# A hybrid recurrence and attention layer: the stores of two stages leave SyncE for the engines that make their data, and three prompt columns of the front move from VectorE to ScalarE

## The chip, the cores and the metric

One core of one Trainium2 chip runs the whole program in a single launch. The metric is the device time of one execution in microseconds (us). Three timed executions of the kernel before took 2099.51, 2095.64 and 2098.21 us; the median is 2098.21 us. A further execution ran under the profiler and took 2093.83 us; every row of the trace is from that one.

Engine names: PE is TensorE, DVE is VectorE, ACT is ScalarE, POOL is GpSimd, SP is SyncE. A DMA is started by an engine's instruction stream: SP, ACT and POOL each have one, and each works its instructions off in order. A DMA instruction whose semaphore has not come therefore holds up what stands behind it in that stream.

## The reference, cut to what matters

The kernel computes one layer of a diffusion backbone in float32, for 1024 latent tokens and 256 prompt tokens of width 1024:

```
h = rms_norm(x) * (1 + sc1) + sh1
z = h @ w_in                      # hq, hf_fwd, hf_bwd, hi, hg, aq, ak, av, gl
q, k = rms_norm per head of aq, ak (latents: rotary positions too)
o_a = softmax(q k^T / 8) v        # latents: cached context keys and latent keys; prompt: prompt keys
f = lb + (1 - lb) * sigmoid(hf)   # gates of the recurrence, both directions
o_h = chunked gated linear recurrence(hq, f, hi), forward + backward; final state is an output
o_h = rms_norm(o_h) * silu(hg)
x = x + g1 * ((sigmoid(gl)[0] * (o_h @ w_ho) + sigmoid(gl)[1] * (o_a @ w_ao)) @ w_out)
x = x + g2 * (square(relu(norm(x) @ w_ff1)) @ w_ff2);   y = rms_norm(x)
```

The shifts, scales and gates (sh, sc, g) are products of a conditioning vector with `w_ada`, one for latents and one for the prompt. Outputs are both y, the prompt's keys and values, and the prompt's final states.

## The kernel before

Tokens are held in three tiles t: t = 0 and 1 are 512 latents each, t = 2 is the 256 prompt tokens. A float32 product is made of three matmuls on operands split in two parts (a rounded high part `hi` made by ACT, and `lo = x - hi` made by DVE): hi*hi, hi*lo, lo*hi. So each column of activations and each block of weights needs one ACT and one DVE instruction before PE can use it. `split` (L283 on ACT, L284 on DVE) does it for weights.

The stages, in order of time in the trace:

- **Front (to about 125 us).** For each tile t and each of eight columns kc (128 of the 1024 channels), PE transposes the tokens (L263), `norm1_col` makes `hs` (the hi part, ACT L272), the whole value `xnb` (ACT L276, or DVE L274 where kc % 3 == 1) and the lo part (DVE L277), and `front_z` multiplies with the weights of the second half of q, and of k and v (L561, L562, L565). Normalisation and rotary positions of q and k (`qk_norm`, L397 to L418) and the splits `qst` and `kst` run on ACT, DVE and POOL beside it. In tile 2 two sets of weights for the first half of q are split as well (`w_aq`, tile `wq`). The L565 matmul of a column needs `hs` of L277; L329 to L331 behind the last column need the `wq` splits.
- **Attention (125 to about 735 us).** First the other half of q (`z_tok`). Then units of one head and 256 queries go through scores (L697), exponentials (ACT L708), normalisation of `pexp` by POOL or DVE in turn (L716), transposes (L738), splits (`pTh`, `pTl`), and values (L754, output `oa` L763). A `Filler` puts the projections for the recurrence between these: QD, FD, VD, GD are scratch tensors in DRAM that `hq_consume`, `hf_consume`, `hi_consume` and `hg_consume` store (tile `ze`), OA takes the outputs of attention.
- **Recurrence (735 to about 1010 us).** 24 units of one head, direction and tile. `prep` loads `uf`, `uq`, `uv`, `ug` from FD, QD, VD, GD, and DVE and POOL make the decays (DVE scans L874 to L880, POOL L883 and L911, both L907). Then PE transposes the keys (`keys_t`, L936), multiplies scores (L947), states (L959; DVE L968 carries them on) and outputs. The gate projections `gl` are the filler here, stored to GT.
- **Projections and MLP (from about 1010 us).** These load OH, OA and GT, and then work through the output projection, the first and the second feed-forward product.

Every instruction's place in its engine's stream is decided before the run: a scheduler lists instructions in program order, moved ahead by `tc.high_priority(offset=...)` by so many places. The splits of `wq` stand in such a block with offset 600, as do the instructions of `norm1_col`.

A store by `dma` (L101) is an instruction of SP, by `store` (L104) one of POOL. Before the change SP issues all loads, and all stores of attention and recurrence. `with_ada` puts the products with `w_ada` (matmuls L181, ACT L183, then `late`: matmuls L188 and ACT L191) between the filler's projections; each `late` waits in the list `todo` for the next projection.

## Time and profile before

| | us |
|---|---|
| median of three timed executions | 2098.21 (2095.64 to 2099.51) |
| the profiled execution, device time | 2093.83 |
| its span in the trace | 2092.1 |
| PE busy in the span | 2035.8 |
| DVE busy | 1405.6 |
| ACT busy | 952.0 |
| POOL busy | 540.3 |

The span is the time from the first to the last instruction in the trace; 1.73 us lie around it. Issuing a DMA is not counted as busy. A row of the timeline gives the start in us, the duration in us, the engine, the line, the operation, the tile written and the tiles read, how many alike instructions follow each other, and in brackets the idle time ahead of it and what ended that. Durations of instructions that follow each other overlap a little: the step from start to start is what one costs its engine. PEclk is the share of full speed granted to PE.

### The profile page before, as it was taken

The page shows a single profiled execution, that of the slowest core. Times are in us where ns is not written, and L with a number is a line of the kernel's source. Part 1 is how long each engine was busy: PE and PEld are TensorE (multiplying, and loading weights), DVE is VectorE, ACT ScalarE, POOL GpSimd, SP SyncE. Part 2 cuts the span into 40 slices and gives each one's busy share as a digit, 9 for nine tenths or more (in the row PEclk, how much of TensorE's full clock was granted, in tenths as well). Part 3 has the DMA queues.
Part 4 walks back from the last instruction along what each step waited for, and adds up shares of the span by engine and source line. Part 5 has one row for each costly group of instructions (what it writes and reads, how often), then busy time and mean ns, then how long its engine had stood idle before and what let it go on. Part 6 is the DMA issues. An engine that isn't in the chain of part 4 may idle for free.

```text
span 2092.1 us, 33337 instructions
## 1 busy us (share of the span) xinstructions
PE 2035.8 (97%) x12244; PEld 1748.0 (84%) x12244; DVE 1405.6 (67%) x2653; ACT 952.0 (46%) x1961; POOL 540.3 (26%) x577
## 2 busy tenths in 40 slices
PE   6899999999999999999999999999999999999998
PEld 4788889988889978888888888988888888888876
DVE  4784676776776797778354735776666666577686
ACT  4754555555565522322231425654454544333442
POOL 1472232333323355455212200222211210000010
PEclk9999999999999999999999999999999999999999
DMA  9455220232221355445644523774444479545773
GB/s 295 130 165 168 74 76 31 77 116 69 78 74 37 107 164 175 139 146 158 216 145 140 206 101 99 218 215 149 157 146 156 157 254 365 166 154 177 228 252 124
DMA packets 230243, 319.19 MB, mean 153 GB/s; under 512 B 18072, under 2 KB 148720, under 8 KB 230080
## 3 DMA queue, kind: packets, MB, share of 16 engines
q1 hardware_dynamic: 217664, 277.41, 41.4%
q0 software_dynamic: 12416, 39.66, 5.3%
q8 instruction: 96, 1.57, 0.3%
q14 instruction: 67, 0.55, 0.1%
HBM read 229.43 MB, written 87.57 MB: 152 GB/s over the span
## 4 chain that ended last, share of the span: by engine, by line
PE 83%; DVE 8%; DMA 5%; ACT 2%; issue 1%; SPq 0%; POOL 0%; DVEq 0%; POOLq 0%; ACTq 0%
PE ps_g L312 7%; PE ps_g L314 7%; PE ps_g L313 7%; PE ps_s L697 4%; PE ps_t L738 4%; PE ps_g L1591 2%; PE ps_g L1589 2%; PE ps_g L1590 2%; PE ps_g L754 2%; PE ps_s L1437 2%; PE ps_s L1438 2%; PE ps_s L1439 2%; DMA wraw<-in_w_ff 2%; PE ps_g L329 2%; PE ps_g L753 2%; PE ps_g L331 2%
## 5 line engine op out<-in xcount | busy, mean ns | idle before, releaser
L312 PE MATMUL ps_g<-hs,wsp 128*128 128x512 f32 (+1 forms) x896 | 322.3, 360 | 0.1
L314 PE MATMUL ps_g<-hs,wsp 128*128 128x512 f32 (+1 forms) x896 | 309.5, 345 | 0.8 <-DVE wsp L284 0.8
L313 PE MATMUL ps_g<-hs,wsp 128*128 128x512 f32 (+1 forms) x896 | 309.0, 345 | 0.0
L716 POOL TENSOR_SCALAR pexp<-pexp,rs 128x512 f32<-128x512 f32 (+1 forms) x104 | 170.2, 1643 | 375.6 <-ACT pTh L741 190.8
L283 ACT ACTIVATE wsp<-wraw 128x1024 fp32r<-128x1024 f32 x110 | 109.6, 998 | 262.8 <-PE ps_g L313 81.0
L284 DVE TENSOR_TENSOR wsp<-wraw,wsp 128x1024 fp32r<-128x1024 f32 x110 | 134.3, 1223 | 120.8 <-ACT wsp L283 120.4
L314 PEld LDWEIGHTS ps_g<-hs,wsp 128*128 128x128 f32 x896 | 169.3, 189 | 22.7 <-DVE wsp L284 1.0
L312 PEld LDWEIGHTS ps_g<-hs,wsp 128*128 128x128 f32 x896 | 169.7, 189 | 21.2 <-issue 4.6
L313 PEld LDWEIGHTS ps_g<-hs,wsp 128*128 128x128 f32 x896 | 170.0, 190 | 15.3
L741 ACT ACTIVATE pTh<-ps_t 128x512 fp32r<-128x512 f32 x200 | 118.9, 601 | 122.3 <-PE ps_t L738 119.3
L698 DVE TENSOR_REDUCE mx<-ps_s 128x1 f32<-128x512 f32 (+1 forms) x208 | 137.0, 663 | 53.9 <-PE ps_s L697 53.4
L283 ACT ACTIVATE ah<-ar 128x640 fp32r<-128x640 f32 (+1 forms) x112 | 80.9, 723 | 187.4 <-PE ps_g L1590 102.3
L708 ACT ACTIVATE pexp<-ps_s,ngm 128x512 f32<-128x512 f32 (+1 forms) x208 | 137.4, 669 | 43.2 <-DVE ngm L702 41.7
L742 DVE TENSOR_TENSOR pTl<-ps_t,pTh 128x512 fp32r<-128x512 f32 x200 | 136.0, 681 | 15.8 <-ACT pTh L741 15.4
L284 DVE TENSOR_TENSOR ah<-ar,ah 128x640 fp32r<-128x640 f32 (+1 forms) x112 | 90.1, 805 | 77.2 <-ACT ah L283 76.0
L697 PE MATMUL ps_s<-Kl,Ql 128*128 128x512 f32 (+1 forms) x416 | 128.9, 415 | 1.6 <-ACT pexp L708 1.6
L738 PE MATMUL ps_t<-ident,pexp 128*128 128x128 f32 x800 | 120.7, 273 | 2.5 <-DVE ngm L702 1.3
L329 PE MATMUL ps_g<-wsp,hs 128*128 128x256 f32 x400 | 117.5, 294 | 0.0
L331 PE MATMUL ps_g<-wsp,hs 128*128 128x256 f32 x400 | 113.7, 284 | 0.0
L330 PE MATMUL ps_g<-wsp,hs 128*128 128x256 f32 x400 | 113.6, 284 | 0.0
L754 PE MATMUL ps_g<-pTl,Vl 128*128 128x256 f32 x400 | 106.2, 286 | 3.6 <-DVE pTl L742 3.5
L753 PE MATMUL ps_g<-pTh,Vl 128*128 128x256 f32 x400 | 106.1, 285 | 1.3 <-DVE oa L763 1.1
(417 smaller groups left out, 5443.5 us busy)
## 6 DMA issues: line engine op xcount, KB each, us to landing
ar<-AF SPq DMA_DIRECT2D x112, 320.0 KB, 3.5
wraw<-in_w_ff SPq DMA_DIRECT2D x32, 1024.0 KB, 6.4
wr<-in_w_ff SPq DMA_DIRECT2D x128, 256.0 KB, 4.5
wraw<-in_w_in SPq DMA_DIRECT2D x18, 1024.0 KB, 5.5
wraw<-in_w_ada SPq DMA_DIRECT2D x16, 1024.0 KB, 5.5
AF<-a POOLq DMA_DIRECT2D x48, 256.0 KB, 2.8
AF<-t POOLq DMA_DIRECT2D x48, 256.0 KB, 2.3
wa<-in_w_ada SPq DMA_DIRECT2D x32, 256.0 KB, 5.8
```

The lines of the kernel that those rows point to most:

```text
L283: s_.activation(hi, raw, AF.Copy)
L284: v.tensor_tensor(lo, raw, f32(hi), op=ALU.subtract)
L312: pe.matmul(out, hi[:, k, :], mh, start=(first and k == 0), stop=False)
L313: pe.matmul(out, hi[:, k, :], ml, start=False, stop=False)
L314: pe.matmul(out, lo[:, k, :], mh, start=False, stop=(last and k == kcs - 1))
L329: pe.matmul(po[:, bb, :], mh[:, off:off + P], wh[:, k % 4, :], start=(k == 0), stop=False)
L331: pe.matmul(po[:, bb, :], ml[:, off:off + P], wh[:, k % 4, :], start=False, stop=(k == KC - 1))
L697: pe.matmul(pq[:, 0:n], self.qh[:, q0:q0 + P], K[self.g][var][self.kts[i]], start=(var == 0), stop=(var == 1))
L716: NORM[(i + j) % len(NORM)].tensor_scalar(x, x, self.rs[j], None, op0=ALU.mult)
L738: pe.transpose(pt[:, a, j * P:(j + 1) * P], self.Ps[j][i][:, b * P:(b + 1) * P], ident)
L753: pe.matmul(pv[:, 0:256], V[self.g][kg][:, b, :], hi[:, a, :], start=(k == 0), stop=False)
L754: pe.matmul(pv[:, 0:256], V[self.g][kg][:, b, :], lo[:, a, :], start=False, stop=(k == last))
```

## The change

Four things are changed.

1. Stores in attention and recurrence no longer go through SP. POOL issues those of OA (12), FD (24), GD (10) and the final states (8), in all 54. ACT issues those of QD (12), VD (10), OH (12) and GT (48), in all 82, by a new helper `store_act`. SP keeps all loads, and the stores of KS, VS, QS, of the caches and of X.
2. In `norm1_col` the columns kc = 1, 4, 7 of the prompt tile (t = 2) have `xnb` made by ACT, no longer by DVE.
3. The splits of `wq` have offset 0 in place of 600.
4. `with_ada` no longer ends attention's filler with the last `late`; it is taken by the first projection of the recurrence's filler.

```diff
+    def store_act(out, in_):
+
+        s_.dma_start(out=f32(out), in_=f32(in_))
...
-            if kc % 3 == 1:
+
+            if kc % 3 == 1 and t < 2:
                 v.tensor_scalar(xn[:, 0:n], pt[:, 0:n], sc, sh, op0=ALU.mult, op1=ALU.add)
             else:
                 s_.activation(xn[:, 0:n], pt[:, 0:n], AF.Identity, scale=sc, bias=sh)
...
-            with tc.high_priority(offset=600):
+            with tc.high_priority(offset=0):
                 for j in range(2):
                     split(*[x[:, 2 * j:2 * j + 2] for x in w_aq[-1]], raw_aq[kc - 4 + j])
...
-                dma(OA[self.h // 2][self.t], o_at[self.h // 2, self.t][:, 0:n])
+                store(OA[self.h // 2][self.t], o_at[self.h // 2, self.t][:, 0:n])
...
-            dma(QD[2 * c + half][t], e[:, 0:n])
+            store_act(QD[2 * c + half][t], e[:, 0:n])
...
-            dma(FD[d][h][t], e[:, 0:n])
+            store(FD[d][h][t], e[:, 0:n])
...
-            dma(VD[c][pr // 2][:, 2 * (pr % 2):2 * (pr % 2) + 2], e)
+            store_act(VD[c][pr // 2][:, 2 * (pr % 2):2 * (pr % 2) + 2], e)
...
-            dma(GD[c][pr // 2][:, 2 * (pr % 2):2 * (pr % 2) + 2], e.rearrange("p (b h) d -> p b (h d)", b=2))
+            store(GD[c][pr // 2][:, 2 * (pr % 2):2 * (pr % 2) + 2], e.rearrange("p (b h) d -> p b (h d)", b=2))
...
-            dma(OH[self.h][self.t], e[:, 0:nb].rearrange("p b d -> p (b d)"))
+            store_act(OH[self.h][self.t], e[:, 0:nb].rearrange("p b d -> p (b d)"))
...
-                    dma(O["new_state_hgrn"][u.d, u.h], st)
+                    store(O["new_state_hgrn"][u.d, u.h], st)
...
-            dma(GT[2 * c + half][t], e[:, 0:n])
+            store_act(GT[2 * c + half][t], e[:, 0:n])
...
-        if todo:
+        if todo and b0:
             todo.pop()()
```

The added lines shift the line numbers of the changed kernel: lines 106 to 272 of before are 4 higher, those from 273 on 5 higher.

The stream of DVE in the front, before, from the last but one column's lo part (first row, L277) to the first `qst`; the last column's lo part is row 134, its `xnb` row 128, the splits of `wq` (L284) rows 129 and 131:

```order
125 L277 TENSOR_TENSOR hs<-xnb,hs 128x256
126 L411 TENSOR_TENSOR qa<-qn,cosb 128x256 x2
127 L403 TENSOR_TENSOR qn<-qn,kwb 128x256
128 L274 TENSOR_SCALAR xnb<-ps_t,s_132,modc 128x256
129 L284 TENSOR_TENSOR wsp<-wq,wsp 128x512
130 L411 TENSOR_TENSOR qa<-qn,cosb 128x128
131 L284 TENSOR_TENSOR wsp<-wq,wsp 128x512
132 L411 TENSOR_TENSOR qa<-qn,cosb 128x128
133 L402 TENSOR_TENSOR qn<-qe,qrst 128x512
134 L277 TENSOR_TENSOR hs<-xnb,hs 128x256
135 L403 TENSOR_TENSOR qn<-qn,qwb 128x512
136 L418 TENSOR_TENSOR qa<-qa,qb 128x256
```

The same place in the changed kernel (the lo parts are L282 now, the `wq` splits L289):

```order
121 L404 TENSOR_REDUCE qss<-sq 128x8
122 L416 TENSOR_TENSOR qa<-qn,cosb 128x256 x2
123 L408 TENSOR_TENSOR qn<-qn,kwb 128x256
124 L282 TENSOR_TENSOR hs<-xnb,hs 128x256 x2
125 L169 TENSOR_SCALAR ms<-qss 128x8
126 L289 TENSOR_TENSOR wsp<-wq,wsp 128x512
127 L416 TENSOR_TENSOR qa<-qn,cosb 128x128 x2
128 L289 TENSOR_TENSOR wsp<-wq,wsp 128x512
129 L485 TENSOR_TENSOR qst<-qa,qst 128x4x64
130 L423 TENSOR_TENSOR qa<-qa,qb 128x256
```

The last two lo parts follow each other directly, ahead of the last two `wq` splits; `xnb` is gone from DVE.

The stream of POOL where the recurrence begins, before (`uf`, `usf`, `uw` are tiles of a unit's `prep`, `ze` with L851 the GD data; row 80 is the L911 of the second unit):

```order
76 L911 TENSOR_TENSOR usf<-uf,usf 128x512
77 L907 TENSOR_TENSOR uw<-uq,um 128x512 x2
78 L907 TENSOR_TENSOR uf<-usf,um 128x512
79 L883 TENSOR_SCALAR uf<-uf 128x512
80 L911 TENSOR_TENSOR usf<-uf,usf 128x512
81 L891 MEMSET um 128x4x16
82 L907 TENSOR_TENSOR uf<-usf,um 128x512
83 L907 TENSOR_TENSOR uw<-uq,um 128x512 x2
84 L851 TENSOR_TENSOR ze<-ze,hnb 128x512
```

And in the changed kernel, with the stores (L104 DMA) that POOL issues between:

```order
146 L916 TENSOR_TENSOR usf<-uf,usf 128x512
147 L104 DMA GD_1_1973<-ze 128x512
148 L912 TENSOR_TENSOR uw<-uq,um 128x512 x2
149 L912 TENSOR_TENSOR uf<-usf,um 128x512
150 L104 DMA OA_2_1905<-oa 128x256
151 L888 TENSOR_SCALAR uf<-uf 128x512
152 L104 DMA OA_2_1908<-oa 128x256
153 L916 TENSOR_TENSOR usf<-uf,usf 128x512
154 L912 TENSOR_TENSOR uw<-uq,um 128x512 x2
155 L896 MEMSET um 128x4x16
156 L856 TENSOR_TENSOR ze<-ze,hnb 128x512
157 L912 TENSOR_TENSOR uf<-usf,um 128x512
```

A store of OA stands between the two instructions that make the second unit's `usf`, and its `uf` of L912 now comes behind `uw` and `ze`.

DVE's stream at the same place, before, around the `usf` (L907) of the first unit, which PE's first key transposes read:

```order
994 L284 TENSOR_TENSOR wsp<-wraw,wsp 128x1024
995 L892 COPY um<-ucp 128x4x3
996 L893 TENSOR_TENSOR um<-ucp 128x4x2
997 L763 TENSOR_TENSOR oa<-ps_g,pvt 64x256
998 L907 TENSOR_TENSOR usf<-usf,um 128x512
999 L896 COPY um<-ucp 128x4
1000 L899 RECIPROCAL um<-ucp 128x4x4
1001 L917 TENSOR_TENSOR uq<-uq,ucp 128x512
```

And in the changed kernel:

```order
990 L289 TENSOR_TENSOR wsp<-wraw,wsp 128x1024
991 L897 COPY um<-ucp 128x4x3
992 L898 TENSOR_TENSOR um<-ucp 128x4x2
993 L901 COPY um<-ucp 128x4
994 L768 TENSOR_TENSOR oa<-ps_g,pvt 64x256
995 L904 RECIPROCAL um<-ucp 128x4x4
996 L922 TENSOR_TENSOR uq<-uq,ucp 128x512
997 L912 TENSOR_TENSOR usf<-usf,um 128x512
```

Three instructions of the second unit (the copy, the reciprocal and `uq`) moved ahead of the first unit's `usf`.

## Rows read from the trace of the kernel before

**Rows 1.** The profile page, its first part: busy us of each engine, share of the span, instructions.

```profile
PE 2035.8 (97%) x12244; PEld 1748.0 (84%) x12244; DVE 1405.6 (67%) x2653; ACT 952.0 (46%) x1961; POOL 540.3 (26%) x577
```

**Rows 2.** Busy time of the engines in stretches of the program. Columns: stretch and its length, busy us and instructions of PE, PE weight load, DVE, ACT, POOL, then PEclk, DMA share, GB/s.

```profile
100.00:125.00 25.00, 20.17 (x106) 16.76 (x105) 24.21 (x56) 16.82 (x42) 18.24 (x23) 0.86 0.61 180
125.00:735.00 610.00, 603.50 (x4251) 545.24 (x4250) 417.25 (x897) 341.55 (x806) 206.30 (x139) 1.00 0.27 86
735.00:775.00 40.00, 35.22 (x267) 29.73 (x265) 39.37 (x69) 10.27 (x19) 23.96 (x24) 0.96 0.52 171
775.00:1010.00 235.00, 232.63 (x1889) 196.02 (x1887) 186.21 (x438) 64.03 (x166) 123.17 (x145) 1.00 0.51 161
...
1300.00:1420.00 120.00, 115.13 (x851) 109.43 (x849) 91.37 (x148) 74.89 (x132) 27.69 (x39) 1.00 0.70 213
```

**Rows 3.** What PE waited for over the whole span: us in total, times, longest us.

```profile
PE ps_s L565 <- DVE hs L277: 4.3, 2, 3.5
PE ps_t L263 <- ACT xnb L276: 4.0, 2, 2.9
...
PE ps_t L936 <- DVE usf L907: 3.5, 2, 1.9
```

**Rows 4.** What SP's stream waited for, in the same form (the row of the FD data).

```profile
SPq L101 <- DVE ze L833: 177.6, 21, 15.5
```

**Rows 5.** The end of the front in stretches of 3 us, columns as in rows 2.

```profile
110.00:113.00 3.00, 3.00 (x17) 2.47 (x16) 3.00 (x7) 1.75 (x3) 3.00 (x5) 1.00 0.97 293
113.00:116.00 3.00, 1.44 (x7) 0.86 (x5) 3.00 (x6) 1.22 (x2) 3.00 (x4) 1.00 0.50 159
116.00:119.00 3.00, 1.02 (x4) 0.59 (x4) 3.00 (x7) 0.62 (x3) 1.97 (x4) 0.94 0.00 0
119.00:122.00 3.00, 3.00 (x16) 3.00 (x17) 3.00 (x6) 2.35 (x9) 2.92 (x5) 0.50 0.96 309
122.00:125.00 3.00, 3.00 (x27) 3.00 (x27) 2.87 (x10) 1.50 (x5) 1.26 (x2) 0.99 0.93 220
```

**Rows 6.** PE's timeline there: the last full-speed matmul, the two that wait for the last column, and the first of the next product.

```profile
114.06 0.39 PE L562 MATMUL ps_g<-wsp,hs 128*128 128x512 f32 x1
117.98 0.50 PE L565 MATMUL ps_s<-wsp,hs 128*128 128x512 f32 x1 [3.54 <-DVE hs L277]
...
118.88 0.58 PE L329 MATMUL ps_g<-wsp,hs 128*128 128x256 f32 x1
```

**Rows 7.** DVE's timeline there; in the left-out lines DVE has no gap either.

```profile
113.28 0.53 DVE L274 TENSOR_SCALAR xnb<-ps_t,s,modc 128x256 f32<-128x256 f32 x1
113.74 0.68 DVE L284 TENSOR_TENSOR wsp<-wq,wsp 128x512 fp32r<-128x512 f32 x1
114.34 1.35 DVE L411 TENSOR_TENSOR qa<-qn,cosb 128x128 f32<-128x128 f32 x1
115.61 0.80 DVE L284 TENSOR_TENSOR wsp<-wq,wsp 128x512 fp32r<-128x512 f32 x1
...
117.39 0.54 DVE L277 TENSOR_TENSOR hs<-xnb,hs 128x256 fp32r<-128x256 f32 x1
...
118.79 0.68 DVE L480 TENSOR_TENSOR qst<-qa,qst 128x256 fp32r<-128x256 f32 x1
```

**Rows 8.** ACT's timeline in the front: a column's `xnb` of the same size on ACT, the next instruction, and ACT's wait behind it.

```profile
108.55 0.58 ACT L276 ACTIVATE xnb<-ps_t,modc,s 128x256 f32<-128x256 f32 x1
109.05 0.56 ACT L272 ACTIVATE hs<-ps_t,modc,s 128x256 fp32r<-128x256 f32 x1
110.74 0.60 ACT L488 ACTIVATE qT<-ps_t 128x512 fp32r<-128x512 f32 x1 [1.12 <-PE ps_t L485]
```

**Rows 9.** The transposes of `qst` that the product behind the front reaches (PE's timeline), the first of which reads the last row of rows 7.

```profile
126.46 0.45 PE L485 MATMUL ps_t<-ident,qst 128*128 128x128 f32 x4
```

**Rows 10.** DMA instructions by the line of the helper that issues them: count, min/median/max ns of the instruction on its stream, first and last start.

```profile
L101 SPq DMA_DIRECT2D GT<-ze x48: 319/320/601, 760.2 to 1069.2; - x48
...
L104 POOL DMA_DIRECT2D AF<-a x48: 540/540/555, 1404.4 to 1701.4; - x48
```

**Rows 11.** Timelines where the recurrence begins: DVE, then PE.

```profile
749.84 1.30 DVE L907 TENSOR_TENSOR usf<-usf,um 128x512 f32<-128x512 f32 x1
751.06 0.16 DVE L896 COPY um<-ucp 128x4 f32<-128x4 f32 x1
751.14 0.24 DVE L899 RECIPROCAL um<-ucp 128x16 f32<-128x16 f32 x1
751.30 0.62 DVE L917 TENSOR_TENSOR uq<-uq,ucp 128x512 f32<-128x512 f32 x1
...
751.20 0.66 PE L936 MATMUL ps_t<-ident,usf 128*128 128x128 f32 x4 [1.58 <-DVE usf L907]
```

**Rows 12.** Timelines in the recurrence: SP, then DVE, then PE.

```profile
893.24 0.34 SPq L101 DMA_DIRECT2D out_new_state_hgrn<-ust  x1
893.67 0.38 SPq L101 DMA_DIRECT2D uf<-FD  x1
...
896.61 1.23 DVE L878 TENSOR_TENSOR_SCAN ucp<-R,uf 128x512 f32<-128x512 f32 x1 [0.83 <-DMA uf<-FD]
...
902.11 0.63 PE L936 MATMUL ps_t<-ident,usf 128*128 128x128 f32 x4 [1.95 <-DVE usf L907]
```

**Rows 13.** POOL's timeline in attention: a `pexp` of L716 and the wait ahead of it.

```profile
506.70 1.76 POOL L716 TENSOR_SCALAR pexp<-pexp,rs 128x512 f32<-128x512 f32 x1 [3.92 <-ACT pTh L741]
```

## The prediction

> **What bounds the kernel now.** I read the page's busy times first [rows 1]: PE works 2035.8 of 2092.1 us, so all that a change can win without touching the products is 56.3 us of idle PE and what a lowered clock costs. Next I cut the span into the stages that the change touches [rows 2]. PE's idle time is length less busy: 4.83 us in the end of the front (100 to 125, at a granted clock of 0.86), 6.5 us in 610 us of attention, 4.78 us where the recurrence begins (735 to 775), 2.37 us in its rest, 4.87 us in the first feed-forward product. Attention and recurrence, where nearly all the stores are, have 13.65 us together. Third comes the list of what PE waited for [rows 3]. Three rows bear on the change: 4.3 us for the lo parts `hs` of DVE L277, of which one wait is 3.5; 4.0 us for `xnb` of ACT L276, also in the front; 3.5 us for DVE's `usf`, both in the recurrence. No wait there names a store. Fourth, SP's own waits [rows 4]: 177.6 us in 21 waits for the data of the FD stores. It is a long time, but time of a stream, not of PE; it counts only where a load behind such a store is late for PE.
>
> **The front: the last column (edits 2 and 3).** In 110 to 113 PE is full at clock 1.00; in 113 to 119 it works 1.44 and 1.02 of 3 us; then, in 119 to 122, it is full but the granted clock is 0.50, the lower of its two levels (1.2 of 2.4 GHz) [rows 5]. PE's timeline shows why: the last L562 starts at 114.06 and the next instruction, L565, at 117.98, after 3.54 us for `hs` [rows 6]. DVE's timeline shows what it did instead [rows 7]: `xnb` of that column at 113.28, a split of `wq` (0.60 us from start to start), `qa` (1.27), a second split of `wq` (0.73), two more instructions, and only at 117.39 `hs`. DVE had no gap, so this is order and load, not latency.
>
> In the changed order `xnb` is gone from DVE (0.46 us by start to start [rows 7]) and the last two `hs` stand ahead of both splits. The two `hs` stand about where `xnb` stood, and take little more (an `hs` lasts 0.54 us, `xnb` 0.53): the last is done between 113.3 and 114.2, I take 113.6, ahead of the 114.45 (114.06 + 0.39) at which PE has ended its L562 [rows 6]. So the 3.54 us go. What is late next? L329 would start about 0.9 us after L565 (118.88 less 117.98 [rows 6]), near 115.4, and needs the second set of split `wq` only for its fifth of eight blocks, 12 matmuls later; 27 of them go in 3 us at full clock [rows 5], so 1.3 us: near 116.7. Counted from 113.6, one split (0.60), two `qa` (1.27, and 0.4 at most) and the last split (0.73) [rows 7] end near 116.6. That is just in time, an estimate with nothing to spare. Without the idle time there is no reason left in these rows for the lower clock, since it was granted in full until PE had been idle: 3 us at 0.50 are worth 1.5 us. Both together are 5.0 us. Lower bound of the gain is 0 (the wait reappears elsewhere), the upper 5.0. I take 4.4, because a slack of 0.1 us is likely to leave a wait of about half a microsecond.
>
> **The front: the other two columns (edit 2).** ACT gets three `xnb` for 0.5 us each, the step from 108.55 to 109.05 [rows 8]. Behind 109.05 ACT waited 1.12 us, so the last one is hidden by that. The middle one falls where ACT is the engine PE waits for (the 4.0 us of `xnb` L276 [rows 3]), and can cost its 0.5; the first saves DVE 0.5 while PE hangs on DVE's chain, and can win as much. Sum 0, bounds -0.5 to +0.5.
>
> **Attention (edit 1).** It puts 24 FD, 12 OA and 10 GD stores on POOL, and 12 QD and 10 VD stores on ACT. SP took 0.32 us for one [rows 10]; on ACT the nearest price is that of SP, so 22 x 0.32 = 7.0 us in a stage in which ACT works 341.55 of 610 us [rows 2]. On POOL a store of this size took 0.54 us [rows 10], so 46 of them are 25 us; POOL works 206.30 of 610. Both fit in idle time. Added waits: each store on POOL waits for DVE's `ze` or `oa`, and behind it stand the `pexp` of L716, which PE's transposes read. POOL was idle 3.92 us ahead of a `pexp` [rows 13], which is the cover; ACT's stores wait for ACT's own data alone. If one in five of ACT's 22 held up a `pexp` that PE waits for, that is 4 x 0.32 = 1.3 us. On the other side, SP's freed loads could win what they cost PE now, of which rows 3 show nothing. Taken: 0; bounds -0.5 to +1.5.
>
> "Perfetto Trace Analysis" of the Trainium skill (DMA Optimizations) says that it may pay to give inputs to one issuing engine and outputs to another. Against it, the skill's "DMA: Bandwidth & Descriptors" (Issuing engines are not separate DMA queues) says that starting DMAs from several engines saves only the issuing stream's time, because all run on the same 16 DMA engines. The trace agrees with the second in attention, where SP waits 177.6 us [rows 4] and PE for no load; by the first, the third rival below would be the likeliest.
>
> **The start of the recurrence (edits 1 and 4).** DVE works 39.37 of 40 us here [rows 2], so the order on DVE decides. PE's first key transposes wait 1.58 us for `usf`, made at 749.84 [rows 11]. In the changed order a copy, a reciprocal and `uq` come first: 751.06 to 751.92, or 0.86 us by these rows. So L936 starts some 0.8 us later. POOL's OA store between L888 and L916 delays the second unit's `usf` by its wait and 0.54; PE reads it only a unit later. The two L188 that edit 4 takes from ahead of L936 give nothing, as PE waits there anyway. Taken +0.8, bounds 0 (`usf` took 1.30 us beside POOL; later it may take 0.7) and +1.5 (0.86 and a 0.6 us collision again).
>
> **The rest of the recurrence (edit 1).** The other wait for `usf`, 1.95 us at 902.11, goes back to a load [rows 12]: SP issues the store of a final state at 893.24, as soon as DVE has made it, and the load of `uf` behind it at 893.67; DVE waits 0.83 us for that load at 896.61, and is then busy until `usf`. With the store on POOL the load goes as soon as its buffer is free. At least 0.83 us of the 1.95 hang on it, at most all. Against it: POOL now waits for the state, with the L907 behind it that DVE's `usf` needs. Taken -1.0, bounds -1.95 and +1.0. ACT's 60 stores are 60 x 0.32 = 19 us beside 64.03 busy of 235 [rows 2]: nothing.
>
> **The first feed-forward product.** Its instructions stand in another order on DVE and ACT, as the scheduler's places shift. PE is idle 4.87 us there [rows 2]; 0, bounds -1.5 and +1.5.
>
> **The sum.** -4.4 + 0 + 0 + 0.8 - 1.0 + 0 = -4.6 us. The profiled execution, 2093.83 us, is 4.38 under the median of the timed ones, and the sum is made against it: 2089.2 on its scale, and 2098.2 - 4.6 = 2093.6 on the scale of the timed runs. I give the latter. Adding bounds: -5.0 -0.5 -0.5 + 0 - 1.95 - 1.5 = -9.5 and 0 + 0.5 + 1.5 + 1.5 + 1.0 + 1.5 = +6.0.
>
> **Rivals.**
> *The front's wait only moves.* DVE has no gap from 110 to 122 [rows 5], and the edits take three `xnb` of 0.46 us off it; all that was put behind `hs` must be done later. The `wq` splits were in time by 0.1 us in my count; and PE, 5 us earlier, reaches the `qst` transposes of 126.46 [rows 9] near 121.5, with `qst` done at 119.47 before [rows 7]: 2 us in place of 7. If a wait of 3.5 us appears at either, only the clock's part of the gain and the recurrence stay: -4.6 + 3.5 = -1.1, so 2097.1 us. For it: DVE's full stretches. Against it: DVE's next 25 us of the second half of q, of which PE is the bound.
>
> *POOL's head of line in attention* ends slower. Place: the FD stores, which wait for DVE behind ACT. SP stood 8.5 us for one on average (177.6 / 21 [rows 4]). If POOL stood as long, a `pexp` behind it would be late by 8.5 less the cover of 3.92, or 4.6 us, plus the store's 0.54. The point from which it decides is a wait of 3.4 us (3.92 - 0.54). Three such hits among 32 units cost 15 us: 2098.2 - 4.6 + 15 = 2108.6. For it: the streams work in order. Against it: SP came early because it had little else; POOL has 206.30 us of its own work and the stores stand behind the matmuls that make their data.
>
> *SP's freedom is worth more.* All of the 3.5 us for `usf` [rows 3] goes, and loads run ahead so far that the DVE work of the first units starts before attention ends: then -0.8 - 1.6 - 1.0 on top of the sum, -8.0, so 2090.2. Against it: DVE has 0.63 us of free time in the 40 us around the start [rows 2].
>
> *The stores leave SP and nothing follows, the front's order aside*, is the forecast itself with -4.4 + 0.8: 2094.6, inside its own range.
>
> **Chances.** Forecast 0.47, with its own range from 2091 to 2096; the wait moves 0.22; SP's freedom 0.18; POOL's head of line 0.13. About 0.2% (4.2 us) is what a measurement of this kernel tells from no change, so faster begins below 2094.0, close to the forecast. Of the forecast's 0.47 some 0.27 lie below, of SP's freedom 0.17, of the moved wait 0.03: faster 0.47. Slower than 2102.4 is POOL's rival with 0.12 and little else: 0.13; the same 0.40. The range from 2087 to 2101 leaves out most of POOL's rival and a tail of the gain.
>
> **What the profile of the changed kernel would show.** Right: in the front no PE wait above 1 us on the lo part L282, and clock 1.00 from 110 to 125; PE's first L936 wait some 0.8 us longer; the 1.95 us wait shorter. SP's list no longer names `ze` and `oa`, POOL's does. Wrong: a PE wait of over 1 us on `qst` or a `wq` split, or one on `pexp` of POOL in attention, behind a DMA of L104. The whole would be wrong if PE's idle time in attention and recurrence (13.65 us) changed by more than 3 us in either direction.

## The result and the profile after

The change made the kernel slower: 2105.2 us, the median of six executions (2103.98 to 2105.92), against 2097.02 us for the kernel before on the same chip (2094.2 to 2099.51). The ratio is 1.0038, 95% interval 1.0027 to 1.005: 8 us, between 5.7 and 10.5. Forecast were 2093.6 us, with a range from 2087 to 2101.

The profiled execution after took 2105.22 us, its span is 2103.4. Against the 2092.1 of the profile before, which lies at the low end of that kernel's times, that is 11.3 us, and these I take apart. The page's first part, to be read against [rows 1]:

```profile
PE 2036.3 (97%) x12244; PEld 1747.4 (83%) x12244; DVE 1404.2 (67%) x2650; ACT 953.1 (45%) x1964; POOL 570.1 (27%) x631
```

PE has the same 12,244 matmuls and works 0.5 us more, so the loss is time in which PE stands. POOL has 54 instructions more, its new stores: other than on SP and ACT, the issuing of a DMA does count as busy on POOL, which works 29.8 us more (0.55 us for each).

PE issues the same matmuls in both kernels in the same order (but for two of L188 that edit 4 moves), so the traces can be laid side by side: the start of the n-th matmul in one, less its start in the other. The table below cuts that difference at fixed matmuls, named by the time at which they start in the trace before. A plus is time lost against the trace before. Its kernels are those of the experiments that follow; the row "after" says where the 11.3 us are.

| us | to 96.6 | front, to 123.6 | attention, to 732.6 | start of recurrence, to 789.2 | its rest, to 1000.0 | to 1457.4 | to 2083.6 | behind the last matmul |
|---|---|---|---|---|---|---|---|---|
| after | -0.9 | -3.7 | -0.8 | +6.8 | +4.9 | +0.9 | +0.6 | +3.5 |
| e1_front_only | -1.2 | -3.7 | -1.7 | +1.6 | +1.7 | +2.6 | -0.4 | 0 |
| e2_no_pool_stores | -3.0 | -3.7 | -1.5 | +2.1 | +6.3 | +2.5 | -1.0 | 0 |
| e3_gd_on_sp | -0.8 | -3.7 | +0.6 | +2.3 | +7.4 | +1.2 | -1.2 | +2.7 |
| e4_oa_on_sp | -2.9 | -3.7 | -1.5 | +2.6 | +6.6 | +5.2 | -0.1 | +2.9 |
| e5_no_act_stores | -2.6 | -3.7 | -1.2 | +5.5 | +2.5 | +1.1 | -1.1 | +3.5 |
| e6_late_back | -0.7 | -3.7 | -1.2 | +5.6 | +6.7 | +2.3 | -1.1 | +3.5 |
| e7_front_a_on_act | -1.1 | -3.7 | -0.4 | 0 | +0.6 | +1.2 | +0.1 | +2.5 |
| e8_fd_alone_on_pool | -0.9 | -3.7 | +1.4 | +0.4 | +5.5 | +2.0 | -0.8 | +1.2 |
| e9_26_on_act | -3.4 | -3.8 | -0.8 | +1.4 | +2.1 | +2.7 | +1.8 | +4.3 |
| e10_32_on_act | +0.4 | -3.7 | -0.6 | +1.3 | +1.9 | +2.1 | +0.5 | +4.3 |
| e11_edit3_alone | -0.9 | +1.3 | -0.3 | +1.6 | +2.3 | -0.3 | -0.2 | 0 |
| e12_20_off_pool | -0.2 | -3.7 | -2.4 | +1.7 | +2.5 | +3.4 | +1.2 | -0.2 |

How fine may this be read? The first column compares mostly the same instructions and spreads by 3.8 us. e11 has the order of before in attention and recurrence, and still loses 1.6 and 2.3 there against that one profile: differences of 2 us in a stage are noise, mostly single stretches at the lower clock that one execution has and another has not. The front's column and the last one repeat to 0.1 us where the kernels agree.

**The front gained.** Stretches of the trace after, as in [rows 2, 5]:

```profile
100.00:125.00 25.00, 21.93 (x145) 18.99 (x146) 22.74 (x57) 18.29 (x45) 17.74 (x24) 1.00 0.76 235
119.00:122.00 3.00, 3.00 (x30) 3.00 (x28) 3.00 (x11) 2.01 (x6) 2.10 (x3) 1.00 0.99 323
```

The granted clock is 1.00 throughout (0.86 before, where two stretches of 3.4 us at 0.50 lie, from 101.6 and from 118.7; the first of them does not matter to the gain, since e8 has one there too and gains the same 3.7 us). What PE still waited for between 100 and 125 (us in total, times, longest):

```profile
PE ps_t L267 <- ACT xnb L281: 2.3, 3, 1.2
PE ps_s L570 <- DVE hs L282: 1.6, 1, 1.6
```

and the rows of POOL, DVE and PE that answer to [rows 6, 7, 9]:

```profile
111.78 1.28 POOL L423 TENSOR_TENSOR qa<-qa,qb 128x512 f32<-128x512 f32 x1 [0.79 <-ACT wsp L288]
111.87 1.94 DVE L282 TENSOR_TENSOR hs<-xnb,hs 128x256 fp32r<-128x256 f32 x2
113.40 0.50 PE L570 MATMUL ps_s<-wsp,hs 128*128 128x512 f32 x1 [1.57 <-DVE hs L282]
114.91 0.39 PE L570 MATMUL ps_s<-wsp,hs 128*128 128x512 f32 x1
121.85 0.46 PE L490 MATMUL ps_t<-ident,qst 128*128 128x128 f32 x4
```

The wait of 3.54 us is gone: the last column's L570 is the one at 114.91, which did not wait. The 1.57 us are a new wait, of the column before it. Its `hs` is the first of the two of the second row and took 1.48 us of the 1.94, beside POOL's L423; in the trace before it took 0.41, at 111.67. No wait for a split of `wq` or for `qst` came.

**The start of the recurrence lost.** The stage of [rows 11] as a stretch, with two 3 us stretches inside it:

```profile
735.00:775.00 40.00, 32.10 (x228) 26.94 (x229) 36.25 (x64) 8.85 (x16) 23.97 (x25) 0.87 0.45 149
744.00:747.00 3.00, 0.00 (x0) 0.00 (x0) 2.94 (x7) 0.00 (x0) 2.04 (x4) 1.00 0.81 264
750.00:753.00 3.00, 3.00 (x10) 2.45 (x9) 3.00 (x5) 1.30 (x2) 2.71 (x3) 0.50 1.09 357
```

Here PE has a stretch with no matmul at all, and then one at half the clock with 10. The timelines of DVE, POOL and PE say why:

```profile
744.94 0.63 DVE L922 TENSOR_TENSOR uq<-uq,ucp 128x512 f32<-128x512 f32 x1
745.04 0.59 POOL L104 DMA_DIRECT2D OA<-oa  x1 [0.93 <-DVE um L904]
745.48 4.01 DVE L912 TENSOR_TENSOR usf<-usf,um 128x512 f32<-128x512 f32 x1
745.65 1.27 POOL L916 TENSOR_TENSOR usf<-uf,usf 128x512 f32<-128x512 f32 x1
746.88 2.05 POOL L912 TENSOR_TENSOR uw<-uq,um 128x512 f32<-128x512 f32 x2
749.55 1.12 PE L941 MATMUL ps_t<-ident,usf 128*128 128x128 f32 x4 [6.25 <-DVE usf L912]
```

`usf`, 1.30 us in [rows 11], lasted 4.01. Read the ends: POOL's L916 began 0.17 us after it and POOL's two `uw` followed without a gap until 748.93; DVE's instruction ended at 749.49, 0.56 us behind POOL's last. That is close to the 0.68 us that the same instruction takes elsewhere: it made hardly any progress as long as POOL worked.

**The rest of the recurrence lost.** What PE waited for between 775 and 1010 (before: one wait for `usf`, the 1.95 us of [rows 12]):

```profile
PE ps_t L941 <- DVE usf L912: 4.7, 2, 3.0
PE ps_s L964 <- issue: 1.7, 2, 1.3
```

The first of the two waits for `usf` is that of [rows 12], now 1.71 us long at 905.09. The load ahead of it did move, and DVE does not wait for it any more:

```profile
888.65 0.32 SPq L101 DMA_DIRECT2D uf<-FD  x1
899.49 1.23 DVE L883 TENSOR_TENSOR_SCAN ucp<-R,uf 128x512 f32<-128x512 f32 x1
```

But DVE was busy until 899.45 with its own work, above all four `uo`, and began this scan only 0.2 us sooner than before, counted from the matmuls of PE ahead of it. PE gained no more than that.

The row of L964 is two waits, 1.27 us at 839.90 and 0.41 at 896.58, for which the profile names nothing. PE's L964 begins 0.1 us behind DVE's last `ust` there, and at 839.90 `usf` stands ahead of that `ust` where it stood behind it before. Against the trace before the two cost 1.2 and 0.6 us.

The second wait for `usf` is new and costs 3.2 us. PE and then DVE around it:

```profile
975.21 0.63 PE L941 MATMUL ps_t<-ident,usf 128*128 128x128 f32 x4 [3.02 <-DVE usf L912]
```

```profile
962.22 1.16 DVE L169 TENSOR_SCALAR ms<-oss 128x4 f32<-128x4 f32 x1
...
966.18 3.24 DVE L1007 SCALAR_TENSOR_TENSOR uo<-uo,orst,ug 128x128 f32<-128x128 f32 x4
...
972.36 0.68 DVE L922 TENSOR_TENSOR uq<-uq,ucp 128x512 f32<-128x512 f32 x1
...
974.38 0.68 DVE L912 TENSOR_TENSOR usf<-usf,um 128x512 f32<-128x512 f32 x1
```

The same place in the trace before, PE's matmul, which did not wait, and DVE:

```profile
968.87 0.63 PE L936 MATMUL ps_t<-ident,usf 128*128 128x128 f32 x4
...
956.96 0.14 DVE L165 TENSOR_SCALAR ms<-oss 128x4 f32<-128x4 f32 x1
...
968.05 0.68 DVE L907 TENSOR_TENSOR usf<-usf,um 128x512 f32<-128x512 f32 x1
...
969.81 0.68 DVE L917 TENSOR_TENSOR uq<-uq,ucp 128x512 f32<-128x512 f32 x1
```

DVE's order changed, though none of its instructions in this stage was edited: the normalisation's `ms` stands later, and `uq` now ahead of `usf` where it stood behind. With the stores on other engines the scheduler lays the instructions out anew.

**Behind the last matmul 3.5 us were lost.** The last data instructions of the trace after, POOL's and SP's, and the DRAIN instructions with which a program closes (count, min/median/max ns, first and last start):

```profile
2094.62 0.55 POOL L170 TENSOR_TENSOR frst<-ms,mexp 128x1 f32<-128x1 f32 x1 [4.23 <-DVE ms L169]
2095.99 1.00 SPq L101 DMA_DIRECT2D out_y_prompt<-x  x2
```

```profile
L1788 POOLq DRAIN  x3: 46/98/8017, 2094.6 to 2103.1; - x3
L1788 SPq DRAIN  x3: 7/7/7, 2098.9 to 2102.9; - x3
```

The same in the trace before:

```profile
2086.81 0.55 POOL L166 TENSOR_TENSOR frst<-ms,mexp 128x1 f32<-128x1 f32 x1 [4.21 <-DVE ms L165]
2088.18 0.99 SPq L101 DMA_DIRECT2D out_y_prompt<-x  x2
```

```profile
L1783 POOLq DRAIN  x3: 46/98/3033, 2086.8 to 2091.8; - x3
L1783 SPq DRAIN  x3: 7/7/7, 2091.2 to 2091.5; - x3
```

POOL's last arithmetic and SP's last store lie alike, 7.8 us later. But the first of POOL's closing DRAINs takes 8.02 us instead of 3.03. Before, it ended at 2089.8 and SP was the last to begin its own, at 2091.2, after its last stores had landed. Now SP is there at 2098.9 and the program waits until 2102.6 for POOL.

### The profile page after: what moved, and what is told of

Same layout as the page of the kernel before. It is cut to its first block, busy times and chain, and to the rows that moved or that the text cites. A ratio compares the mean times of both kernels' runs of the same rounds, so it can differ in the third digit from the quotient of the medians.

```text
span 2103.4 us, 33287 instructions
## 1 busy us (share of the span) xinstructions
PE 2036.3 (97%) x12244; PEld 1747.4 (83%) x12244; DVE 1404.2 (67%) x2650; ACT 953.1 (45%) x1964; POOL 570.1 (27%) x631
## 3 DMA queue, kind: packets, MB, share of 16 engines
q8 instruction: 96, 1.57, 0.3%
## 4 chain that ended last, share of the span: by engine, by line
PE 82%; DVE 9%; DMA 5%; ACT 3%; issue 2%; SPq 0%; POOL 0%; DVEq 0%; POOLq 0%; ACTq 0%
PE ps_g L317 7%; PE ps_g L319 6%; PE ps_g L318 6%; PE ps_s L702 4%; PE ps_t L743 3%; PE ps_g L1596 2%; PE ps_g L1594 2%; PE ps_g L1595 2%; PE ps_s L1442 2%; PE ps_s L1444 2%; PE ps_s L1443 2%; PE ps_g L759 2%; DMA wraw<-in_w_ff 2%; PE ps_g L334 2%; PE ps_s L1594 2%; PE ps_s L1595 2%
## 5 line engine op out<-in xcount | busy, mean ns | idle before, releaser
L289 DVE TENSOR_TENSOR wsp<-wraw,wsp 128x1024 fp32r<-128x1024 f32 x110 | 135.9, 1237 | 120.6 <-ACT wsp L288 120.2
L289 DVE TENSOR_TENSOR ah<-ar,ah 128x640 fp32r<-128x640 f32 (+1 forms) x112 | 89.8, 801 | 79.4 <-ACT ah L288 77.5
L170 POOL TENSOR_TENSOR frst<-ms,mexp 128x1 f32<-128x1 f32 x10 | 11.4, 1150 | 364.8 <-DVE ssf L1683 279.0
```

The lines of the kernel that those rows point to most:

```text
L289: v.tensor_tensor(lo, raw, f32(hi), op=ALU.subtract)
```

## The experiments

All are compared by their profile with the trace before (the table above). Those in several rounds were also timed against the kernel before on the same chip.

### The front's edits alone, and all but POOL's stores

e1_front_only is the kernel before with edits 2 and 3:

```diff
-            if kc % 3 == 1:
+            if kc % 3 == 1 and t < 2:
-            with tc.high_priority(offset=600):
+            with tc.high_priority(offset=0):
```

> The kernel before with the edits 2 and 3 alone (three prompt columns on ScalarE, the wq splits at offset 0); all stores on SP, the late of the conditioning where it was. Theory: the front gains about 4.8 us, the loss is all in what the stores do. Then every matmul behind the front comes 4 to 5.5 us earlier than in the kernel before, to the end: about 2092.5 us beside 2097. Rival: the front's gain is given back later whatever the stores do; then the end is within 1 us of the kernel before.

Measured: 2091.91 us, median of ten, against 2094.15; ratio 0.9985, interval 0.9974 to 0.9995. The front gains 3.7 us, as in the changed kernel, the end is unchanged. Its waits for `usf` between 700 and 1010 are 4.5 us in two, the longest 2.3. The ratio is a gain of 3.1 us (1.0 to 5.4), where the theory gave 4 to 5.5. So the front's edits are a gain, and the loss is in the rest of the change.

e2_no_pool_stores is the changed kernel with OA, FD, GD and the final states on SP again; ACT keeps its 82:

```diff
-                store(OA[self.h // 2][self.t], o_at[self.h // 2, self.t][:, 0:n])
+                dma(OA[self.h // 2][self.t], o_at[self.h // 2, self.t][:, 0:n])
```

and the same for the three others.

> The changed kernel, but OA, FD, GD and the final states (54 stores) again on SP; the 82 stores on ScalarE stay. Theory: the 54 stores on GpSimd cost all that was lost behind attention, the start of the recurrence first (6.6 us there, 5 more in the recurrence). Then PE's first L941 waits under 2.5 us and the end is 4 to 6 us ahead of the kernel before: about 2092 us. Rival: ScalarE's stores, or loads that run ahead on a freed SP, cost the time; then the loss stays by half or more: above 2099 us.

Measured: 2095.36 against 2094.15, ratio 1.0002 (0.999 to 1.0015). The start of the recurrence and the end are back at e1's values; the rest of the recurrence loses 6.3 us, 4.0 of them between 962 and 1000. The theory (POOL's stores cost all of it, 2092) fell, and so did the rival's 2099; PE's first L941 waits 3.5 us, not under 2.5. ACT's stores, with edit 4, thus cost what the front wins. By the timed ratios they cost some 3.5 us (1.0002 less 0.9985), and POOL's 54 stores 7.5 (1.0038 less 1.0002), each give or take 3.5 as the intervals have it. The Trainium skill's "DMA: Bandwidth & Descriptors" (Issuing engines are not separate DMA queues) lets one expect no faster transfers from another issuer; the trace agrees, as 82 stores taken off SP made no stage faster.

### The start of the recurrence: which store?

e3_gd_on_sp puts the 10 GD stores back (`dma(GD[...` for `store(GD[...`), e4_oa_on_sp the 12 OA stores. All else is as in the changed kernel.

> The changed kernel, but the 10 GD stores again on SP. In the list of instructions the first unit's usf on VectorE then stands ahead of uq again, as in the kernel before; GpSimd still has the OA store ahead of its L916. Theory (order): usf took 4.01 us because it came behind uq, whose end let GpSimd start two uw at the same time, and waited for them; then usf takes 0.7 to 1.4 us here and PE's first L941 waits under 2.5 us instead of 6.25. Rival (the OA store): GpSimd's L916 is late by the store ahead of it and falls on usf; then usf takes over 2.5 us and the wait stays above 4 us.

Measured: 2102.28 us (one execution; before 2094.15). The stage loses 2.3 us, near the 1.6 of e1. DVE, POOL and PE in e3:

```profile
745.26 1.31 DVE L912 TENSOR_TENSOR usf<-usf,um 128x512 f32<-128x512 f32 x1
745.97 0.59 POOL L104 DMA_DIRECT2D OA<-oa  x1
746.63 1.12 PE L941 MATMUL ps_t<-ident,usf 128*128 128x128 f32 x4 [3.48 <-DVE usf L912]
```

`usf` is back at 1.31 us and ahead of `uq`; PE's wait, 3.48, stayed above what the theory gave (e1, where the two L188 of edit 4 stand ahead of it, waits 2.3).

> The changed kernel, but the 12 OA stores again on SP. VectorE's order stays that of the changed kernel (usf behind uq), and no store stands ahead of GpSimd's L916. Theory (order): usf still takes over 2.5 us and PE's first L941 still waits over 4 us. Rival (the OA store): usf takes 0.7 to 1.4 us and the wait falls below 2.5 us.

Measured: 2102.97 us (one). In e4, POOL and DVE and then PE:

```profile
741.23 1.26 POOL L916 TENSOR_TENSOR usf<-uf,usf 128x512 f32<-128x512 f32 x1
742.96 0.68 DVE L912 TENSOR_TENSOR usf<-usf,um 128x512 f32<-128x512 f32 x1
743.18 2.38 POOL L912 TENSOR_TENSOR uw<-uq,um 128x512 f32<-128x512 f32 x2 [0.69 <-DVE uq L922]
743.69 1.11 PE L941 MATMUL ps_t<-ident,usf 128*128 128x128 f32 x4 [4.07 <-DVE usf L912]
```

My theory, that the order (`usf` behind `uq`, which comes with GD on POOL) alone makes `usf` long, fell: here the order is the new one, and `usf` takes 0.68 us. The rival's wait (under 2.5) was missed too, at 4.07. Together the two runs say that it needs both: GD on POOL puts `usf` behind `uq`, and the OA store, with its wait of 0.93 us, holds POOL's L916 back until it meets that later `usf`. With either one undone the loss is 2.3 or 2.6 instead of 6.8. Each kernel has one profile here, but the length of `usf` repeats: 4.01 us in after, e5 and e6, 1.30 or 1.31 in the ten others, and 0.68 in e4. "SBUF — State Buffer" of the Trainium skill (SBUF: two separate sides) says that DVE and GpSimd share a pair of ports as an exclusive lock: whichever starts first holds it for its whole instruction, and the other stands still. The 4.01 us agree as to standing still, but not as to the order: by the trace DVE's `usf` started 0.17 us ahead of POOL's L916, and over three POOL instructions in a row DVE did not get in between. Why POOL won each time isn't shown.

e6_late_back undoes edit 4 alone:

```diff
-        if todo and b0:
+        if todo:
```

> The changed kernel, but the last late of the conditioning again ends attention's filler (edit 4 undone). Theory: it moves two short matmuls and changes nothing by itself: every step of PE within 0.7 us of the changed kernel, the start of the recurrence still at over 5 us lost. Rival: these matmuls filled part of PE's wait there and their move is part of the loss; then PE's first L941 wait falls by the 1 us and more that they take.

Measured: 2105.11 us (one; before 2095.32). The stage loses 5.6 us instead of 6.8, PE's wait is 4.12 instead of 6.25, and `usf` lasts 4.01 as before. I had given edit 4 no effect; the theory's 0.7 us a step did not hold, and the wait fell as the rival said. With their own wait of 0.55 us for ACT the two L188 fill 1.2 us of it when they stand ahead of it. The rest: PE comes to it 0.7 us later, out of a longer stretch at the lower clock, and `usf` comes 0.3 us sooner. But the matmuls must be done in either place, and 1.2 us of the stage in one profile of each is within the noise. Open, therefore; at most a small term.

### The rest of the recurrence: ACT's stores or POOL's?

e5_no_act_stores has QD, VD, OH and GT on SP again:

```diff
-            store_act(QD[2 * c + half][t], e[:, 0:n])
+            dma(QD[2 * c + half][t], e[:, 0:n])
```

> The changed kernel, but QD, VD, OH and GT (82 stores) again on SP; the 54 stores on GpSimd stay. Theory: the loss of 3.2 us near 969 us of the trace (PE's L941 waiting for usf) comes from the other order on VectorE that the stores on ScalarE brought there, as it also stands in the kernel with these stores alone; then that step is under 0.7 us here, while the start of the recurrence still loses 5 us or more (the GpSimd stores are the same). Rival: the final states on GpSimd make the loss near 969; then it stays above 2.5 us.

Measured: 2097.87 us (one; before 2095.32). The start of the recurrence loses 5.5 us, as expected. Between 962 and 1000 it loses 1.4, between the two that the theory and the rival gave. e8_fd_alone_on_pool keeps ACT's stores and leaves POOL the 24 FD alone (OA, GD and the states back on SP):

> The changed kernel with OA, GD and the final states again on SP: of the 54 stores the 24 of FD stay on GpSimd, ScalarE keeps its 82. Theory by terms: front 3.7 us gained; start of the recurrence 2 to 2.6 us lost, as in the kernels without GD or OA on GpSimd; 0 near 848 us; 3 to 4 us lost near 969; closing DRAIN 5.2 us (184 DMAs), so 2.2 us more than before at the end. Rival: FD stores on GpSimd hold up pexp in attention; then PE loses over 1 us between 150 and 720 us, which none of the four runs showed but by a single step of 1.55 us at 250 us in one.

Measured: 2098.93 us (one). On PE, DVE, ACT and POOL its trace has the same order of instructions as e2's, stores aside: the 24 FD stores on POOL moved nothing. The start of the recurrence loses 0.4, less than the 2 to 2.6 expected, its rest 5.5, of which 3.9 lie between 962 and 1000, and the end 1.2 (2.2 expected); PE's waits in e8 between 735 and 1010:

```profile
PE ps_t L941 <- DVE usf L912: 4.9, 2, 3.0
PE ps_t L1013 <- DVE uo L1007: 1.8, 1, 1.8
```

Over all runs the stretch from 962 to 1000 loses 3.3 to 5.0 us in the six kernels with stores on ACT in the recurrence (after, e2, e3, e4, e6, e8), 1.4 in e5, and 0 to 0.4 in the six without either. It is not one wait in all of them: after, e3, e4 and e6 wait 3.0 us for `usf`, e2 and e8 1.9 and 1.8 us for `uo`, a little earlier, and e5 1.3 us ahead of the same L941. All but after and e5 then have a stretch at a clock of 0.50, worth 1.7. Without that the loss is 3.3 us with the stores on both engines, 2.3 with ACT's (e2, e8), 1.4 with POOL's (e5): the larger part comes with ACT's stores. What is common is DVE's new order there; that it is the cause was not tried with ACT's stores kept and the old order forced.

The 1.2 us of L964 near 839.90 stand in after and in e3 to e6 (0.9 to 1.2), and in no other kernel: they come with POOL's stores other than FD's, and the final states are the only ones that all five have there. They alone were not tried. The 0.6 us at 896.58 stand in the six kernels with ACT's stores (0.5 to 0.7). In attention the FD stores on POOL took 1.4 in e8 against -1.7 in e1; e8 has one stretch at 0.50 there that is worth 1.7, and after, with the same stores and more, has -0.8. That is no loss I can tell from noise.

### The end: does POOL's DRAIN count its DMAs?

e7_front_a_on_act is e1 with 48 stores of a later stage (lines 1484 to 1488, the AFD stores of B11, B22 and B21) moved from POOL to ACT; nothing in attention or recurrence is touched:

```diff
-        store(AFD[i][:, FI["B11"], 0:512], a11)
+        store_act(AFD[i][:, FI["B11"], 0:512], a11)
```

> The kernel before with edits 2 and 3, and 48 of the feed-forward stores (B11, B22, B21) issued by ScalarE in place of GpSimd, so that GpSimd issues 112 DMAs in place of 160. Theory: GpSimd's closing DRAIN grows by some 0.09 us for each DMA beyond about 133 that it has issued (3.03 us at 160, 6.95 at 202, 7.20 at 204, 8.02 at 214); then it takes under 0.7 us here behind the last POOL work, and the end after the last matmul falls from 8.05 to 5.3 to 6 us: 2 us less than with edits 2 and 3 alone. Rival: the DRAIN hangs on something else of those kernels (the stores in attention and recurrence, not their number); then it stays at 3.0 us.

Measured: 2095.04 us, median of eleven, against 2095.32; ratio 1.0003 (0.9993 to 1.0012). By the theory the long DRAIN should have been gone with fewer DMAs. It is there:

```profile
L1786 POOLq DRAIN  x3: 46/93/7034, 2083.4 to 2091.0; - x3
```

A simple "more DMAs, longer DRAIN" was refuted. Against the number of DMAs on POOL, relative to before, all kernels of the study gave (longest DRAIN, us): -48: 7.03 (e7); 0: 3.03 (before, e1, e2, e11); +24: 5.65 (e8); +42: 6.95 (e4); +44: 7.20 (e3); +54: 8.02 (after, e5, e6). (The expectations count 160 DMAs of POOL for the kernel before; the trace has 165, and all other counts there are 5 higher too.) From 0 to +54 that is (8.02 - 3.03) / 54 = 0.09 us for each DMA. If the count starts anew somewhere below 0, -48 fits with the same slope. Two kernels look for the restart: e10_32_on_act moves B21 and B11 (32 stores), e9_26_on_act B21 and the first ten B11 (26).

> As the run with 26, but 32 stores (all of B21 and B11) on ScalarE: 128 DMAs on GpSimd. Theory (round a ring of about 92): the DRAIN has just started again from its high value: 8 to 9 us, and the end after the last matmul 11.5 to 12.5 us. Rival (it only falls with the number): under 1 us.

Measured: 2100.03 us (one; before 2096.35); DRAIN 8.34 us, as expected.

> The kernel before with edits 2 and 3, and 26 of the feed-forward stores (16 of B21, 10 of B11) issued by ScalarE, so that GpSimd issues 134 DMAs. The closing DRAIN of GpSimd took 3.03 us at 160 DMAs, then 5.65, 6.95, 7.20, 8.02 at 184, 202, 204, 214 (0.092 us each), but 7.03 at 112. Theory: it falls by 0.092 us for each DMA taken away until it is used up, and then starts again from a high value, as if what the software queue has to clear were counted round a ring of about 92; 0.58 us of it is the last POOL work. Then it takes 0.6 to 1.0 us here, and the end after the last matmul is 5.3 to 6 us in place of 8.05. Rival: it depends on which stores there are, not on their number; then it lies anywhere, above 2.5 us.

Measured: 2098.53 against 2096.35, ratio 1.0009 (0.9997 to 1.0021); DRAIN 8.83 us: the restart lies above -26, not below as I had placed it. e12_20_off_pool moves 20 (ten of B21 to ACT, ten other stores to SP, by `put=dma` in the helper `final`).

> The kernel before with edits 2 and 3, and 20 stores fewer on GpSimd: the first 10 of B21 on ScalarE and the 10 of the outputs that GpSimd had on SP. It issues 20 DMAs fewer than the kernel before. The closing DRAIN so far, by DMAs more or less than the kernel before: -48: 7.03; -32: 8.34; -26: 8.83; 0: 3.03; +24: 5.65; +42: 6.95; +44: 7.20; +54: 8.02 us. Theory (a sawtooth round a ring of some 90 DMAs, which starts again just above -26): here it takes 0.6 to 1.8 us and the end after the last matmul is 5.3 to 6.9 us, against 8.05. Then the kernel is 1 to 3 us faster than with the front's edits alone. Rival (no sawtooth; stores of the feed-forward part taken from GpSimd lengthen it): 4 us or more.

Measured: 2092.6 against 2095.39, ratio 0.9988 (0.9978 to 0.9998). DRAIN in e12, POOL and SP:

```profile
L1786 POOLq DRAIN  x3: 46/93/1401, 2089.2 to 2094.0; - x3
L1786 SPq DRAIN  x3: 7/7/130, 2093.4 to 2094.0; - x3
```

1.40 us, as the slope has it for 20 fewer than 0 (3.03 - 20 x 0.09 = 1.2), so the restart lies between -26 and -20. The end of the program did not shorten (-0.2): SP, whose wait for the last stores lasts until 2093.4, bounds it. So the end and the gain of 1 to 3 us over e1 that the theory gave did not come. Behind before's DRAIN there were 1.4 us to SP's (2091.2 less 2089.8), so some 15 more DMAs would have stayed hidden; beyond, each costs 0.09 us. e12 is not better than e1, whose front it shares.

### Edit 3 alone

e11_edit3_alone is the kernel before with the offset of the `wq` splits at 0, without edit 2.

> The kernel before with edit 3 alone (wq splits at offset 0). In its list the last column's lo part still stands behind all wq splits, as before; with edit 2 alone the list of every engine is the same as with both. Theory: edit 2 makes the whole gain of the front; then here PE still waits 2.5 us or more for the last lo part and the step of the front is within 1 us of the kernel before. Rival: the offset frees the lo parts; then PE waits under 2 us and the front gains over 2 us.

Measured: 2097.35 us (one; before 2096.35). The front loses 1.3 us. What PE waited for in e11 between 88 and 125:

```profile
PE ps_s L565 <- DVE hs L277: 3.7, 1, 3.7
PE ps_t L263 <- DVE xnb L274: 1.5, 1, 1.5
```

The 3.5 us wait is there as before. And with edit 2 alone every engine's list of instructions comes out the same as in e1, as the expectation says, so edit 3 does nothing beside edit 2, and nothing good without it: the gain is all of edit 2. This rests on the lists; edit 2 alone was not run.

The fastest kernel measured is e1, faster than both: 0.9985 of before (e12, at 0.9988, can't be told from it).

## Why the prediction was wrong, and where it was right

**The front (-4.4): right, with one wait misplaced.** It gained 3.7 in every kernel with edit 2. `xnb` off DVE took the wait of 3.54 away and the clock stayed up. I left 0.6 us for a wait on the `wq` splits, and none came. The wait that did come, 1.57 us, is one column earlier: I moved two `hs` together and followed the last one only. The first of them had stood three instructions further ahead in DVE's stream, and now it fell beside POOL's L423 and took 1.48 us, not 0.54. I also credited the gain to edits 2 and 3; it is edit 2's. The rival that the wait moves to `wq` or `qst` is refuted; a smaller one that I had not named came true.

**Attention (0): right.** POOL waited for the data of its stores, as the rival said, but little. POOL's waits in the trace after, 125 to 735:

```profile
POOL FD L104 <- DVE ze L838: 18.0, 12, 5.5
...
POOL OA L104 <- PE ps_t L743: 14.5, 3, 5.2
...
POOL OA L104 <- DVE oa L768: 10.4, 5, 4.4
```

SP's 8.5 us a wait was no guide for POOL: it arrives later, and waits 2.1 us on average in these three rows (42.9 / 20). At least three waits (5.5, 5.2 and 4.4) passed the 3.4 us from which I let the rival decide, PE waited for no `pexp` of POOL, and the stage took no longer (-0.8, within the noise).

**The start of the recurrence (+0.8): wrong by 6.0.** The failing step is the collision of DVE and POOL. I had `usf` later by 0.86 us, which is what the order made of it: less the 5.4 us gained before it, 749.84 becomes 744.4, and it began at 745.48, 1.0 later. I wrote that the second unit's `usf` on POOL would be late by the OA store, and that "PE reads it only a unit later", and left it there. But it was this shift that laid POOL's L916 and `uw` onto DVE's `usf`: 4.01 us instead of 1.30, 2.7 more, where my upper bound allowed 0.6 for a collision. The rest is the clock, for which I had no term here. Behind the wait of 6.25 us PE goes on at 749.55, and the granted clock is 0.50 from 748.3 to 755.1: 5.6 us of work at half the clock lose 2.8. (The stretches at 0.50 ahead of the wait, 3.4 us from 738.1 after and from 743.3 before, cost nothing by themselves, because PE then waits for DVE.) Together 1.0 + 2.7 + 2.8 = 6.5, measured 6.8.

**The rest of the recurrence (-1.0): wrong by 5.9.** Two steps failed. I wrote that at least 0.83 of the 1.95 us hang on the load behind a store. The load moved and DVE's 0.83 us of waiting went, but PE's wait became 1.71, 0.24 less: DVE's own work was nearly as late. And ACT's 60 stores I took for "nothing" because ACT had the time, and POOL's for +1.0 at most. Of the 4.9 us, 3.3 lie between 962 and 1000 (2.3 in the kernels with ACT's stores alone), 1.2 at 839.90 with POOL's stores, and 0.6 at 896.58 with ACT's. I priced the instruction (0.32 us each) and not what the scheduler does with it: DVE's order changed, and PE waits for DVE here. That the order is the cause is argued from these rows, not tried.

**The end (no term): 3.5 missing.** My sum does not have the end of the program at all. POOL's DRAIN of 3.03 us stood in the trace before, hidden; 54 more DMAs on its queue brought it out. Nothing there showed that its length goes with the DMAs, but the stretch itself could have been listed among the bounds.

**First feed-forward product (0) and the others:** +0.9 and +0.6 here, within what one profile can tell. But the twelve kernels with edit 2 all lose 0.9 us or more between 1000 and 1457, and e11, without it, does not (-0.3): about 1 us of the front's gain seems to be given back there. Why was not followed.

By stage the forecast's -4.6 thus becomes -3.7 - 0.8 + 6.8 + 4.9 + 0.9 on the same stages, +8.1, and with the first stretch (-0.9), the last (+0.6) and the end (+3.5) the 11.3 us of the profiles. My last sentence, that the whole is wrong if PE's idle time in attention and recurrence changes by more than 3 us, is what came about: between the same matmuls it rose by 7.9 us, and the stages lost 10.9. Of the other signs, the clock of 1.00 in the front came; a wait above 1 us on L282 did too, against the forecast. The bounds, added up, end at +6.0, or 2104.2; I gave 2101, and the measured time lies above both. The rival of SP's freedom is refuted (no stage won by it); the slower rival had the right sign in the wrong stage, with another mechanism.

## What to carry to other kernels

A store that moves into the stream of a computing engine is an instruction of that engine: it can shift what follows it and, under a scheduler, what stands on other engines (the FD stores moved nothing, those of GD and OA a good deal); price it by the new order, around the place where the engine that bounds the kernel waits, and not by its own 0.3 to 0.6 us. Where DVE and POOL both work on the same unit, look at which POOL instructions come to lie on the one DVE instruction that TensorE waits for. And when queues are changed, read the program's end, too.

## What the runs showed of the hardware that I had not expected

- A DVE instruction of 0.68 us lasted 4.01 beside three POOL instructions in a row (1.27 and two in 2.05 us), in after and, with the same 4.01, in e5 and e6; beside one it lasted 1.30. In the front an `hs` of 0.41 us lasted 1.48 beside one of 1.28.
- POOL's closing DRAIN goes with the number of DMAs that POOL has issued: 0.09 us for each, from 1.40 us (20 fewer than before) to 8.02 (54 more), and 7.03 to 8.83 us for 48 to 26 fewer. The steps fit a count that starts anew after some 90 DMAs (8.83 - 1.40 = 7.4 us is 83 steps, and six DMAs lie between the two kernels); what it counts was not tried.
- A wait of PE is not always followed by the lower clock: before, 1.95 us at 902.11 were followed by a stretch at 1.00, and in e11, with the same order there, 2.16 us at 904.19 by one at 0.54:

```profile
902.00:905.00 3.00, 2.89 (x15) 2.51 (x16) 3.00 (x5) 0.60 (x1) 2.97 (x4) 1.00 0.45 171
```

```profile
905.00:908.00 3.00, 3.00 (x9) 2.27 (x8) 3.00 (x6) 0.46 (x1) 2.06 (x3) 0.54 0.16 59
```

The first is of before, the second of e11. The stretch of 3.4 us at the lower clock cost 1.7 there, most of the 2.3 us that e11 loses in that stage with the order of before.
